# A hybrid mLSTM and attention layer: old keys copied a sequence at a time, products without sigmoids beside the gates, a reciprocal on the Pool engine, and the fourth sum of x on VectorE

## The chip, the cores and the metric

The kernel runs on one core of one Trainium2 chip. A core has a tensor engine for matmuls (TensorE, PE in the profile, with PEld for its weight loads), a vector engine (VectorE, DVE), a scalar engine (ScalarE, ACT), a general engine (GpSimd, POOL) and a sync engine that issues most transfers (SyncE, SP). The engines run side by side, each works through its own instructions in order, and they wait for each other through semaphores. The metric is the device time of one execution in microseconds (us); less is better. Times of several runs are given as a median with the lowest and the highest.

## What is computed

One layer of a decoder, for a prompt of 512 tokens and for 8 sequences with 4 new tokens each (32), so 544 columns in all. The reference, cut to what matters here:

```python
u = x @ w_in                       # 2048 wide x, 13 parts
q_m,k_m,v_m,o_m,z_m, q_a,k_a,v_a,z_a, g_m,g_a, i_pre,f_pre = split(u)
ig = i_pre + b_igate
lf = log_sigmoid(f_pre + b_fgate)  # the gates: 4 heads
h_m, C, n, m = mlstm(q_m, k_m, v_m, ig, lf, C0, n0, m0)   # cumulative sums and maxima of ig, lf
h_a = window_attention(q_a, k_a, v_a, slopes, sinks)      # window of 128, old keys from a buffer
br_m = norm(h_m) * sigmoid(o_m) * silu(z_m)
br_a = h_a * silu(z_a)
y = sigmoid(g_m) * (br_m @ w_proj_m) + sigmoid(g_a) * (br_a @ w_proj_a)
out = layernorm(alpha * x + y @ w_out)
# also returned: C, n, m, and the key and value buffers (the old rows shifted by the new ones)
```

`state_attn_k` and `state_attn_v` hold 128 old rows for each of the 8 sequences; the returned buffers hold their last 124 rows and the 4 new ones.

## The kernel before

**Products in two halves of precision.** Everything is float32, but TensorE works on a rounded form. A weight block `raw` (128 x 1024) is split into a rounded part `wh`, cast on ACT (L198), and a remainder `wl = raw - wh`, subtracted on DVE (L199); x has the same two parts. A plain product (`products`, L207) runs wh with x's high part, wh with its low part and wl with its high part.

**Pairs of products.** Nearly all of `w_in` is multiplied by `paired` (L695 on): two blocks of 128 output columns together as seven products of quarter size, the steps n = 0 to 6 of a pair, in the manner of Strassen and Winograd. Each step is 16 matmuls with wh (L662) and then 8 with wl (L664), into one of three banks. The operands on the x side are the quarters of x and four sums of them, s1, n2, n3 and s4, each in a high and a low part (s1h, s1l and so on). The operands on the weight side are blocks and sums of blocks, which `prepare` makes three steps ahead: sums on DVE (L642), or, for the pairs marked "acc", by a transfer on POOL's queue that adds as it writes (L640). `gather` takes the results out of the banks on ACT, POOL and DVE (L672 to L691): after step 1 it needs POOL for c22 (L681), after step 5 DVE for c12 (L689).

**Order of the work.** First two plain products (the values of attention, 16 + 16 steps of k) with the gates' products between them (`gates_half`, which loads the gates' columns `graw` and writes their parts `wga` and `wgb`; its two matmul lines are L388). Then a list of pairs: the keys KA first, then three from the list `fill`, then sixteen pairs QA/ZA of attention with the rest of `fill` between them. `fill` holds the first seven merge gates, whose results get a sigmoid on ACT and are stored to `d_sgm` and `d_sga`, and then the products of the mLSTM (V, K, Q), which are stored as they are.

**Side work.** `tick()` is called after each step and lets each running generator go on to its next `yield`. There are the gates' chain (`gates`), the transposes of values and keys, the sums of x (`x_sums`), and attention (`attentions`), which begins when the gates' chain has ended. `gates` computes the log sigmoid on four rows of 544 columns: absolute value and exponential on ACT, then on DVE `dd = 2 + e`, its reciprocal (L418), `s = e * dd` (L421), its square (L422), a polynomial in steps of one SCALAR_TENSOR_TENSOR each (L426, L428), then cumulative sums and maxima, exponentials on ACT, and transposes. `x_sums` makes the sums on POOL (L552, and for the fourth L572 and L573) and splits them with `hilo` (L242: a cast on ACT and a subtraction on DVE). The fourth sum `n2r` is made in place over n2 and becomes s4 behind the plain products.

**What sets the order on an engine.** A tile scheduler orders each engine's instructions by priority: the order of the program, moved ahead by `tc.high_priority(offset=...)` (400 for `prepare` and `gather`, 500 for the gates' products) and held back by `tc.issue_after(x)`, which lets work start no earlier in that order than x. So work that is moved in the program also moves other work on the same engine. POOL issues its adding transfers in order with its own operations; SP issues loads and stores in order.

**Table loads.** Where ACT goes from one function to another, the timeline can show a row ACT_TABLE_LOAD ahead of the operation; a group of them is put down to the line of that operation or of one beside it.

Of the kernel before, what the change touches and what calls it, by code (L numbers as in the profile page):

```python
# [21 lines left out]
SEQ = 512  # L22
# [51 lines left out]
def _build(tc, nc, i, o, es):  # L74
# [35 lines left out]
    def r32(ap):  # L110
        return ap.bitcast(F32)
# [172 lines left out]
    def two_k(ch):  # L284
        return slice(ch * 2, ch * 2 + 2)
# [65 lines left out]
    with tc.issue_after(state["load"].ins):  # L351
# [5 lines left out]
        nc.sync.dma_start(sinkb[:], i["attn_sinks"].partition_broadcast(128))  # L357
        nc.sync.dma_start(sinkc[:], i["attn_sinks"].unsqueeze(1).to_broadcast([AH, NTS]))
    G.memset(mh[:], -0.5)
    V.tensor_scalar(ones_r[:], cc[:, 0:2], 0.0, 0.5, op0=ALU.mult, op1=ALU.add)  # L360
    A.copy(sel[:], cc[:, C_SEL:C_SEL + 32])
    for t_ in (row_h, nM):
# [28 lines left out]
    def gates(ps):  # L391
# [23 lines left out]

        dd, s, s2, p, lf = row(), u, u2, row(), row()
        V.tensor_scalar(dd, e_, 2.0, None, op0=ALU.add)
        V.reciprocal(dd, dd)  # L418
        yield
        yield  # L420
        V.tensor_tensor(out=s, in0=e_, in1=dd, op=ALU.mult)  # L421
# [10 lines left out]
        yield  # L432

        rst, c = s, s2
        G.memset(rst, 1.0)
        G.memset(rst[:, 0:SEQ:128], 0.0)
        G.memset(rst[:, SEQ:T:NTS], 0.0)
        V.tensor_tensor_scan(c, rst, lf, 0.0, ALU.mult, ALU.add)
        ap, d0 = lf, row()
        V.tensor_tensor(out=ap, in0=ig, in1=c, op=ALU.subtract)  # L440
        yield
        G.memset(d0, 0.0)
        V.tensor_copy(d0[:, 128:SEQ:128], c[:, 127:SEQ - 1:128])
        V.memset(d0[:, SEQ:T:NTS], NEG)
        am, M = p, fg
# [32 lines left out]
        V.tensor_tensor(out=dc, in0=m0, in1=nMs, op=ALU.add)  # L478
        yield
        yield  # L480
        A.activation(T2[0:4], mrow, AF.Exp, scale=-1.0)
        A.activation(T2[64:68], wl_, AF.Exp)
        A.activation(T2[32:36, SEQ:T], it, AF.Exp)
        A.activation(dc, dc, AF.Exp)
        V.tensor_copy(T1[0:4, :], ap)
# [5 lines left out]
        for q in (32, 64):  # L491
            V.tensor_tensor(out=M, in0=M, in1=r32(nM[q - 32:q - 28]), op=ALU.subtract)
            A.copy(nM[q:q + 4], M)

        reps = []
        for src in (T2, T1):
# [52 lines left out]
    def x_sums():  # L549
        for ch in range(4):  # L550
            ks_ = two_k(ch)
            G.tensor_tensor(out=n2r[:, ks_], in0=n2r[:, ks_], in1=s1r[:, ks_], op=ALU.subtract)  # L552
            if ch % 2:
                yield
        for name, r_ in (("n3", n3r), ("s1", s1r), ("n2", n2r)):
            h_, l_ = S[name] = quad(act2, name)
            for ch in range(4):
                ks_ = two_k(ch)
                if name == "n3":
                    A.activation(h_[:, ks_], r_[:, ks_], AF.Copy, scale=-1.0)  # L560
                    V.scalar_tensor_tensor(l_[:, ks_], r_[:, ks_], -1.0, r32(h_[:, ks_]), op0=ALU.mult, op1=ALU.subtract)
                else:

                    with tc.issue_after(state["x_end"].ins):
                        hilo(r_[:, ks_], h_[:, ks_], l_[:, ks_])
                if ch % 2:
                    yield
        for ch in range(4):
            ks_ = two_k(ch)
            k0 = (ch * 2) % 4  # L570
            h12, l12 = (r32(xk2[p][ch // 2][:, k0:k0 + 2, 0:HT]) for p in range(2))
            G.tensor_tensor(out=n2r[:, ks_], in0=h12, in1=n2r[:, ks_], op=ALU.subtract)  # L572
            G.tensor_tensor(out=n2r[:, ks_], in0=n2r[:, ks_], in1=l12, op=ALU.add)  # L573

        while not state.get("plain_done"):
            yield
        s4 = S["s4"] = quad(act, "s4")
        for ch in range(4):
            ks_ = two_k(ch)
            hilo(n2r[:, ks_], s4[0][:, ks_], s4[1][:, ks_])  # L580
            yield

# [241 lines left out]
    def end_qz(k):  # L824
# [16 lines left out]
            waiting[k] = (qs, sz)  # L841
        return end

    def attentions():
        while gates_ in live:
            yield
        esG.close()
        with tc.issue_after(state["gates_end"].ins):
            V.tensor_scalar(nsinkb[:], sinkb[:], -1.0, None, op0=ALU.mult)
        with tc.issue_after(state["load"].ins):  # L850
            for src, dst in ((d_ks, kb_s), (d_vr[SEQ:T], vb_s)):
                nc.sync.dma_start(dst[:, 124:128].rearrange("b t k d -> b t (k d)"),
                                  src.rearrange("(b t) c -> b t c", t=NTS))
            nc.sync.dma_start(kb_s[:, 0:124], i["state_attn_k"][:, NTS:128])
            nc.sync.dma_start(vb_s[:, 0:124], i["state_attn_v"][:, NTS:128])
        state["ca"] = pool(esP, "ca", 1).tile([128, 388], F32, name="ca")
        with tc.issue_after(state["load"].ins):
            nc.sync.dma_start(state["ca"][:], i["consts"][:, C_DIST:C_DIST + 388])
        open_attention()
        state["open"] = True  # L860
        for k in range(16):
            if k % 4 == 0:
                kv = kv_head(k // 4)
            while k not in waiting:
                yield
            yield
            yield
            yield from attention(k, *waiting.pop(k), kv)
            state["done"] = k + 1
        esB.close()  # L870
        yield from sample_attention()
        esT.close()
        esP.close()
        open_samples()
        state["samples"] = True
# [394 lines left out]

    merge_gates = [pair(GA + ct * 128, GM + ct * 128, end_gates(d_sga, ct, d_sgm, ct)) for ct in range(16)]

    fill = merge_gates[:7] + [w for h in range(2) for w in vkq(h)]
    work = [pair(KA, KA + 128, end_keys)] + [fill.pop(0) for _ in range(3)]
    n_fill = len(fill)
    for k in range(16):
# [585 lines left out]
```

## Time and profile before

| | us |
|---|---|
| median of 3 runs | 2508.42 (2507.06 to 2509.03) |
| the profiled execution, its own time | 2510.34 |
| its span in the profile | 2508.6 |
| mean granted clock of TensorE | 0.997 |

The span reaches from the first to the last instruction that the profiler recorded; the execution's own time is 1.7 us longer. In the page's second part the span is cut into 40 slices of 62.7 us, and a digit is the busy share in tenths:

```profile
PE   8999999999999999999999999999999999999997
DVE  7867677677677677787777888787855654766667
ACT  5557676667667665443433444444633333344431
POOL 5111121121111111121111122211000000110101
```

POOL is used most in the first slice, in which the sums of x are made. Lines of a timeline give the start and the duration in us, the engine, the line of the program, the operation, what it writes and reads, the shape, the count, and in brackets the idle time ahead of it and what ended it. A row of busy time by stage gives the stretch, its length, then for PE, PEld, DVE, ACT and POOL the busy time with the count of instructions, the granted clock, the DMA share and GB/s.

### The profile page before, as it was taken

The numbers are of one execution on the slowest core, as the hardware profiler recorded it, in microseconds if no ns is written. First come the engines' busy times: TensorE is split into PE (matmuls) and PEld (weight loads), VectorE is DVE, ScalarE is ACT, GpSimd is POOL, SyncE is SP. The second block draws the span as 40 slices with busy tenths as digits, with TensorE's granted clock in tenths as the row PEclk, the third lists the DMA queues.
The fourth block names the chain that finished last, engine by engine and source line by source line (L and its number), as shares of the span: only waits on it lengthen the run. The fifth ranks groups of instructions, "written<-read, shape, count | busy, mean of one in ns | idle before, by whom it ended". The sixth has DMA issues, their size and how long they took to land.

```text
span 2508.6 us, 48661 instructions
## 1 busy us (share of the span) xinstructions
PE 2469.9 (98%) x19542; PEld 2411.2 (96%) x19542; DVE 1815.4 (72%) x2773; ACT 1244.6 (50%) x2035; POOL 402.5 (16%) x388
## 2 busy tenths in 40 slices
PE   8999999999999999999999999999999999999997
PEld 7999999999999999999999999999999999999997
DVE  7867677677677677787777888787855654766667
ACT  5557676667667665443433444444633333344431
POOL 5111121121111111121111122211000000110101
PEclk9999999999999999999999999999999999999999
DMA  6676666666666655467667567576745546788776
GB/s 165 152 199 159 158 145 163 152 151 159 153 154 156 152 126 150 106 202 227 193 211 226 164 199 217 172 220 216 247 160 177 188 153 212 209 228 251 209 216 195
DMA packets 551331, 457.35 MB, mean 182 GB/s; under 512 B 44832, under 2 KB 451536, under 8 KB 550816
## 3 DMA queue, kind: packets, MB, share of 16 engines
q1 hardware_dynamic: 534208, 394.73, 53.1%
q0 software_dynamic: 15696, 57.15, 11.7%
q8 instruction: 153, 2.51, 0.4%
q10 hardware_dynamic: 1200, 2.36, 0.3%
q14 instruction: 74, 0.61, 0.1%
HBM read 313.82 MB, written 94.22 MB: 163 GB/s over the span
## 4 chain that ended last, share of the span: by engine, by line
PE 85%; issue 5%; DMA 4%; DVE 2%; ACT 1%; SPq 0%; POOL 0%; DVEq 0%; POOLq 0%; ACTq 0%
PE bank L662 43%; PE bank L664 21%; PE bank L207 6%; PE sm L1366 2%; PE sm L1186 1%; PE sm L1180 1%; PE sm L1398 1%; PE sm L770 1%; PE sm L1411 1%; PE sm L808 1%; PE sm L207 1%; PE sm L798 1%; PE sm L1728 1%; DMA tx<-d_y 1%; DVE wl L199 1%
## 5 line engine op out<-in xcount | busy, mean ns | idle before, releaser
L198 ACT CAST wh<-raw 128x1024 fp32r<-128x1024 f32 x632 | 661.4, 1048 | 815.8 <-PE bank L662 678.0
L199 DVE TENSOR_TENSOR wl<-raw,wh 128x1024 fp32r<-128x1024 f32 x632 | 779.6, 1234 | 239.7 <-ACT wh L198 207.2
L662 PE MATMUL bank<-xk,wh 128*128 128x272 f32 x2336 | 322.7, 288 | 1.7 <-ACT wh L198 1.2
L642 DVE TENSOR_TENSOR raw<-raw,raw 128x1024 f32<-128x1024 f32 x238 | 303.5, 1278 | 14.1 <-DMA raw<-in_w_in 5.4
L662 PEld LDWEIGHTS bank<-xk,wh 128*128 128x128 f32 x2336 | 303.9, 188 | 4.3 <-ACT wh L198 1.7
L681 POOL TENSOR_TENSOR ev<-p,ev 128x272 f32<-128x272 f32 x82 | 121.0, 1476 | 583.6 <-ACT ev L680 533.9
L664 PE MATMUL bank<-xk,wl 128*128 128x272 f32 x1168 | 171.7, 287 | 0.0
L662 PE MATMUL bank<-n3h,wh 128*128 128x272 f32 x656 | 169.2, 289 | 1.6 <-DVE ev L683 1.6
L662 PE MATMUL bank<-s1h,wh 128*128 128x272 f32 x656 | 170.0, 291 | 0.2 <-ACT wh L198 0.2
L662 PE MATMUL bank<-n2h,wh 128*128 128x272 f32 x656 | 168.9, 288 | 1.1 <-ACT wh L198 1.1
L662 PE MATMUL bank<-s4h,wh 128*128 128x272 f32 x656 | 169.3, 290 | 0.4
L662 PE MATMUL bank<-n3l,wh 128*128 128x272 f32 x656 | 169.0, 289 | 0.0
L662 PE MATMUL bank<-n2l,wh 128*128 128x272 f32 x656 | 168.8, 289 | 0.0
L662 PE MATMUL bank<-s1l,wh 128*128 128x272 f32 x656 | 168.5, 289 | 0.0
L662 PE MATMUL bank<-s4l,wh 128*128 128x272 f32 x656 | 168.4, 289 | 0.0
L664 PEld LDWEIGHTS bank<-xk,wl 128*128 128x128 f32 x1168 | 155.8, 188 | 0.0
L662 PE MATMUL bank<-a11h,wh 128*128 128x272 f32 x584 | 150.0, 289 | 0.2 <-ACT wh L198 0.2
L662 PE MATMUL bank<-a11l,wh 128*128 128x272 f32 x584 | 149.9, 289 | 0.0
L207 PE MATMUL bank<-bh,wl 128*128 128x272 f32 x704 | 147.5, 289 | 1.3 <-DVE wl L199 1.3
L207 PE MATMUL bank<-bl,wh 128*128 128x272 f32 x704 | 148.6, 289 | 0.0
L207 PE MATMUL bank<-bh,wh 128*128 128x272 f32 x704 | 148.1, 289 | 0.0
L640 POOL DMA_DIRECT2D raw<-raw x90 | 77.6, 863 | 302.8 <-DVE sums L783 153.0
(489 smaller groups left out, 5640.1 us busy)
## 6 DMA issues: line engine op xcount, KB each, us to landing
raw<-in_w_in SPq DMA_DIRECT2D x296, 512.0 KB, 4.7
raw<-raw POOLq DMA_DIRECT2D x90, 512.0 KB, 5.0
C<-in_state_mlstm_C SPq DMA_DIRECT2D x32, 1024.0 KB, 7.0
out<-C SPq DMA_DIRECT2D x64, 512.0 KB, 3.6
raw<-in_w_proj_a SPq DMA_DIRECT2D x32, 512.0 KB, 7.1
raw<-in_w_proj_m SPq DMA_DIRECT2D x32, 512.0 KB, 5.7
raw<-in_w_out SPq DMA_DIRECT2D x32, 512.0 KB, 5.5
d_sgm<-ev SPq DMA_DIRECT2D x16, 272.0 KB, 8.4
```

What stands on the lines that cost most here:

```text
L198: A.copy(wh[:, k:k + n], raw[:, k:k + n])
L199: V.tensor_tensor(out=wl[:, k:k + n], in0=raw[:, k:k + n], in1=r32(wh[:, k:k + n]), op=ALU.subtract)
L207: PE.matmul(ps[f][:, :w], a[:, kk], b(k, c, w), start=(k == 0 and n == 0), stop=(k == 15 and n == 2))
L640: G.dma_start(out=w[out][:], in_=w[b][:], accum_op=ALU.add)
L642: V.tensor_tensor(out=w[out][:], in0=w[a][:], in1=w[b][:], op=ALU.add)
L662: PE.matmul(ps, wh[:, k], x(p, k), start=(first and k == 0 and p == 0), stop=False, skip_group_check=True)
L664: state["end"] = PE.matmul(ps, wl[:, k], x(0, k), start=False, stop=(k == 7), skip_group_check=True)
L681: G.tensor_tensor(out=c22, in0=p1, in1=c11, op=ALU.subtract)
L770: PE.matmul(pp[:, c0 + w0:c0 + 256], qs[a][:, j * 128:j * 128 + 128], kx[:, k0:k0 + 256 - w0], start=(n == 0), stop=(n == 1))
L798: PE.transpose(pt[:, (m - m0_) * 128:(m - m0_) * 128 + 128], s_[:, b, 128:256] if own else s_[:, b + 1, 0:128], ident)
L808: PE.matmul(po[:, b * 128:b * 128 + n], VA[:, b], p_[:, 2 * b:2 * b + n // 128], start=(b == 0 and m == 0), stop=(b == 3 and m == 1), skip ...
L1366: PE.matmul(pp[:, 0:258], a[:, b * 128:b * 128 + 128], b_[:, b, f], start=(b == 0 and n == 0), stop=(b == 3 and n == 2))
```

## The change

The diff has four parts. **Old rows:** the last 124 old rows of keys and values were copied by two transfers, issued when attention opens; now a generator `old_rows` issues sixteen, one for each sequence and buffer, one in every second tick, each not ahead of the latest weight load. **Fill:** the list now begins with the mLSTM's products of heads 0 and 1, with the seven merge gates put in behind the first three; so the three pairs behind KA are V, V and K and no longer merge gates. **Gates:** the reciprocal becomes a power of -1 on POOL (a two-input operation whose second input is a column of -1.0 in `mh`, broadcast), with one more `yield` behind it; four memsets go from POOL to DVE; two exponentials change places, and a `yield` is added between the copies into `nM`. **Fourth sum:** its eight TENSOR_TENSOR go from POOL to DVE and behind the wait for the plain products' end.

```diff
@@ -357,6 +357,7 @@
         nc.sync.dma_start(sinkb[:], i["attn_sinks"].partition_broadcast(128))
         nc.sync.dma_start(sinkc[:], i["attn_sinks"].unsqueeze(1).to_broadcast([AH, NTS]))
     G.memset(mh[:], -0.5)
+    G.memset(mh[:, 4:8], -1.0)
     V.tensor_scalar(ones_r[:], cc[:, 0:2], 0.0, 0.5, op0=ALU.mult, op1=ALU.add)
     A.copy(sel[:], cc[:, C_SEL:C_SEL + 32])
     for t_ in (row_h, nM):
@@ -415,7 +416,8 @@
 
         dd, s, s2, p, lf = row(), u, u2, row(), row()
         V.tensor_scalar(dd, e_, 2.0, None, op0=ALU.add)
-        V.reciprocal(dd, dd)
+        G.tensor_tensor(out=dd, in0=dd, in1=mh[0:4, 4:5].to_broadcast([4, T]), op=ALU.pow)
+        yield
         yield
         yield
         V.tensor_tensor(out=s, in0=e_, in1=dd, op=ALU.mult)
@@ -432,14 +434,14 @@
         yield
 
         rst, c = s, s2
-        G.memset(rst, 1.0)
-        G.memset(rst[:, 0:SEQ:128], 0.0)
-        G.memset(rst[:, SEQ:T:NTS], 0.0)
+        V.memset(rst, 1.0)
+        V.memset(rst[:, 0:SEQ:128], 0.0)
+        V.memset(rst[:, SEQ:T:NTS], 0.0)
         V.tensor_tensor_scan(c, rst, lf, 0.0, ALU.mult, ALU.add)
         ap, d0 = lf, row()
         V.tensor_tensor(out=ap, in0=ig, in1=c, op=ALU.subtract)
         yield
-        G.memset(d0, 0.0)
+        V.memset(d0, 0.0)
         V.tensor_copy(d0[:, 128:SEQ:128], c[:, 127:SEQ - 1:128])
         V.memset(d0[:, SEQ:T:NTS], NEG)
         am, M = p, fg
@@ -478,8 +480,8 @@
         V.tensor_tensor(out=dc, in0=m0, in1=nMs, op=ALU.add)
         yield
         yield
-        A.activation(T2[0:4], mrow, AF.Exp, scale=-1.0)
-        A.activation(T2[64:68], wl_, AF.Exp)
+        with tc.issue_after(A.activation(T2[64:68], wl_, AF.Exp).ins):
+            A.activation(T2[0:4], mrow, AF.Exp, scale=-1.0)
         A.activation(T2[32:36, SEQ:T], it, AF.Exp)
         A.activation(dc, dc, AF.Exp)
         V.tensor_copy(T1[0:4, :], ap)
@@ -491,6 +493,7 @@
         for q in (32, 64):
             V.tensor_tensor(out=M, in0=M, in1=r32(nM[q - 32:q - 28]), op=ALU.subtract)
             A.copy(nM[q:q + 4], M)
+            yield
 
         reps = []
         for src in (T2, T1):
@@ -565,18 +568,16 @@
                         hilo(r_[:, ks_], h_[:, ks_], l_[:, ks_])
                 if ch % 2:
                     yield
+
+        while not state.get("plain_done"):
+            yield
+        s4 = S["s4"] = quad(act, "s4")
         for ch in range(4):
             ks_ = two_k(ch)
             k0 = (ch * 2) % 4
             h12, l12 = (r32(xk2[p][ch // 2][:, k0:k0 + 2, 0:HT]) for p in range(2))
-            G.tensor_tensor(out=n2r[:, ks_], in0=h12, in1=n2r[:, ks_], op=ALU.subtract)
-            G.tensor_tensor(out=n2r[:, ks_], in0=n2r[:, ks_], in1=l12, op=ALU.add)
-
-        while not state.get("plain_done"):
-            yield
-        s4 = S["s4"] = quad(act, "s4")
-        for ch in range(4):
-            ks_ = two_k(ch)
+            V.tensor_tensor(out=n2r[:, ks_], in0=h12, in1=n2r[:, ks_], op=ALU.subtract)
+            V.tensor_tensor(out=n2r[:, ks_], in0=n2r[:, ks_], in1=l12, op=ALU.add)
             hilo(n2r[:, ks_], s4[0][:, ks_], s4[1][:, ks_])
             yield
 
@@ -841,6 +842,15 @@
             waiting[k] = (qs, sz)
         return end
 
+    def old_rows():
+
+        for dst, src in ((kb_s, i["state_attn_k"]), (vb_s, i["state_attn_v"])):
+            for b in range(NB):
+                with tc.issue_after(state["load"].ins):
+                    nc.sync.dma_start(dst[b, 0:124], src[b, NTS:128])
+                yield
+                yield
+
     def attentions():
         while gates_ in live:
             yield
@@ -851,13 +861,12 @@
             for src, dst in ((d_ks, kb_s), (d_vr[SEQ:T], vb_s)):
                 nc.sync.dma_start(dst[:, 124:128].rearrange("b t k d -> b t (k d)"),
                                   src.rearrange("(b t) c -> b t c", t=NTS))
-            nc.sync.dma_start(kb_s[:, 0:124], i["state_attn_k"][:, NTS:128])
-            nc.sync.dma_start(vb_s[:, 0:124], i["state_attn_v"][:, NTS:128])
         state["ca"] = pool(esP, "ca", 1).tile([128, 388], F32, name="ca")
         with tc.issue_after(state["load"].ins):
             nc.sync.dma_start(state["ca"][:], i["consts"][:, C_DIST:C_DIST + 388])
         open_attention()
         state["open"] = True
+        spawn(old_rows())
         for k in range(16):
             if k % 4 == 0:
                 kv = kv_head(k // 4)
@@ -1270,7 +1279,8 @@
 
     merge_gates = [pair(GA + ct * 128, GM + ct * 128, end_gates(d_sga, ct, d_sgm, ct)) for ct in range(16)]
 
-    fill = merge_gates[:7] + [w for h in range(2) for w in vkq(h)]
+    fill = [w for h in range(2) for w in vkq(h)]
+    fill[3:3] = merge_gates[:7]
     work = [pair(KA, KA + 128, end_keys)] + [fill.pop(0) for _ in range(3)]
     n_fill = len(fill)
     for k in range(16):
```

On DVE around the gates' products, in rows of line, operation, output, inputs and shape, before (n2l is the low part of the sum n2, ev a result on its way out, raw2 a sum of weight blocks, graw the gates' columns):

```order
L242 TENSOR_TENSOR n2l_70_723<-n2r_134,n2h_69_722 128x544 x4
L383 TENSOR_TENSOR wga_55_589<-graw_54_587,wga_55_589 128x8x4 x2
L531 COPY ev_65_703<-sm_63_696 32x128
L199 TENSOR_TENSOR wl_59_634<-raw_57_631,wh_58_633 128x1024
L642 TENSOR_TENSOR raw2_83_775<-raw_77_763,raw_78_765 128x1024
```

And after:

```order
L242 TENSOR_TENSOR n2l_70_724<-n2r_134,n2h_69_723 128x544 x4
L579 TENSOR_TENSOR n2r_134<-xk2_5_115,n2r_134 128x544
L384 TENSOR_TENSOR wga_55_590<-graw_54_588,wga_55_590 128x8x4 x2
L579 TENSOR_TENSOR n2r_134<-xk2_5_115,n2r_134 128x544
L579 TENSOR_TENSOR n2r_134<-xk2_6_116,n2r_134 128x544 x2
L580 TENSOR_TENSOR n2r_134<-n2r_134,xk2_7_117 128x544
L534 COPY ev_65_704<-sm_63_697 32x128
L199 TENSOR_TENSOR wl_59_635<-raw_57_632,wh_58_634 128x1024
L580 TENSOR_TENSOR n2r_134<-n2r_134,xk2_7_117 128x544
L580 TENSOR_TENSOR n2r_134<-n2r_134,xk2_8_118 128x544 x2
L643 TENSOR_TENSOR raw2_83_776<-raw_77_764,raw_78_766 128x1024
```

One of the fourth sum's operations now stands between the four n2l and wga, and the seven others around the split of the last plain product's weights (wl_59).

On DVE in the last steps of the first pair (KA), before: t are the gates' rows; ev_95 and ev_94 are the pair's results, with L687 after step 4, L689 after step 5 and L691 after step 6; wl_111 is the low part for step 6, and wl_115 that for the first step of the next pair:

```order
L444 MEMSET t_135_1157 4x8
L426 SCALAR_TENSOR_TENSOR t_100_882<-t_100_882,t_76_753 4x544 x2
L199 TENSOR_TENSOR wl_111_934<-raw2_80_769,wh_110_933 128x1024
L687 SCALAR_TENSOR_TENSOR ev_95_848<-bank_98_855,ev_95_848 128x272
L531 COPY ev_109_927<-sm_107_920 32x128
L426 SCALAR_TENSOR_TENSOR t_100_882<-t_100_882,t_76_753 4x544
L642 TENSOR_TENSOR raw2_116_999<-raw_104_890,raw_105_892 128x1024
L689 SCALAR_TENSOR_TENSOR ev_95_848<-bank_93_822,ev_95_848 128x272
L199 TENSOR_TENSOR wl_115_969<-raw_104_890,wh_114_968 128x1024
```

And after (L690 is the evacuation after step 5, L423 the product with the reciprocal, L444 and L446 memsets of one row, L428 steps of the polynomial):

```order
L690 SCALAR_TENSOR_TENSOR ev_95_849<-bank_93_823,ev_95_849 128x272
L423 TENSOR_TENSOR t_75_753<-t_90_815,t_99_882 4x544
L688 SCALAR_TENSOR_TENSOR ev_95_849<-bank_98_856,ev_95_849 128x272
L424 TENSOR_TENSOR t_76_754<-t_75_753 4x544
L426 TENSOR_SCALAR t_100_883<-t_76_754 4x544
L432 TENSOR_SCALAR t_101_884<-t_74_752 4x544
L444 MEMSET t_139_1191 4x544
L428 SCALAR_TENSOR_TENSOR t_100_883<-t_100_883,t_76_754 4x544
L446 MEMSET t_139_1191 4x8
L428 SCALAR_TENSOR_TENSOR t_100_883<-t_100_883,t_76_754 4x544 x3
L199 TENSOR_TENSOR wl_111_935<-raw2_80_770,wh_110_934 128x1024
```

Before, wl_111 stood ahead of the evacuation after step 5 (L689), and the product with the reciprocal, L421, stood six rows ahead of the first row shown; now wl_111 stands behind both evacuations (steps 4 and 5) and, from L423 on, ten operations of the gates' chain.

On POOL in the same stretch, from the plain products on, before (xk2 are the parts of x, raw and raw2 are weight blocks and sums, the DMA rows are issues of adding transfers):

```order
L572 TENSOR_TENSOR n2r_134<-xk2_5_115,n2r_134 128x544 x2
L572 TENSOR_TENSOR n2r_134<-xk2_6_116,n2r_134 128x544 x2
L573 TENSOR_TENSOR n2r_134<-n2r_134,xk2_7_117 128x544 x2
L573 TENSOR_TENSOR n2r_134<-n2r_134,xk2_8_118 128x544 x2
L640 DMA raw_78_765<-raw2_79_767 128x1024
L681 TENSOR_TENSOR ev_95_848<-p1_89_812,ev_94_847 128x272
L640 DMA raw2_80_769<-raw_77_763 128x1024
L442 MEMSET t_135_1157 4x544
```

And after:

```order
L377 MEMSET wga_55_590 128x1024
L378 MEMSET wgb_56_591 128x1024
L641 DMA raw_78_766<-raw2_79_768 128x1024
L419 TENSOR_TENSOR t_99_882<-t_99_882,mh_88 4x544
L682 TENSOR_TENSOR ev_95_849<-p1_89_813,ev_94_848 128x272
L641 DMA raw2_80_770<-raw_77_764 128x1024
L458 MEMSET t_146_1265 128x544
```

The sum's operations (L572, L573) are gone from POOL, and the power, L419, stands between the adding transfer for step 4's block, raw_78, and c22 (L682), with the adding transfer for step 6's block, raw2_80, behind both.

4 lines of the change are left out of this document (2 added, 2 removed).

## The prediction

> **What bounds the kernel now.** I read the page first (busy time by engine), then busy time by stage, then what PE waited for, and last the timelines around those waits.
>
> ```profile
> span 2508.6 us, 48661 instructions
> PE 2469.9 (98%) x19542; PEld 2411.2 (96%) x19542; DVE 1815.4 (72%) x2773; ACT 1244.6 (50%) x2035; POOL 402.5 (16%) x388
> ```
>
> TensorE (PE) is busy for all but 38.7 us. An edit that leaves the matmuls alone can only close such holes or open new ones, so the question is where the holes are. By stage (PE's busy time is the third number, PEclk the granted clock):
>
> ```profile
> 45.00:48.70 3.70, 0.15 (x3) 0.06 (x1) 3.70 (x6) 0.93 (x2) 3.70 (x3) 1.00 0.00 0
> 49.50:53.00 3.50, 3.50 (x18) 3.50 (x17) 1.35 (x2) 0.00 (x0) 3.50 (x3) 0.51 0.98 263
> 60.00:95.00 35.00, 34.86 (x279) 34.60 (x278) 31.09 (x42) 16.99 (x23) 7.43 (x11) 1.00 0.61 147
> 95.00:120.00 25.00, 21.70 (x163) 20.38 (x162) 20.84 (x40) 15.51 (x22) 2.64 (x4) 1.00 0.63 149
> 144.00:160.00 16.00, 14.04 (x108) 13.41 (x107) 10.44 (x16) 7.68 (x12) 2.41 (x3) 1.00 0.85 204
> 160.00:2300.00 2140.00, 2136.25 (x17003) 2085.56 (x17002) 1558.99 (x2367) 1091.68 (x1775) 332.53 (x315) 1.00 0.65 181
> 2446.00:2508.60 62.60, 45.93 (x322) 44.26 (x320) 44.80 (x81) 8.63 (x12) 7.17 (x8) 0.91 0.64 195
> ...
> PE bank L388 <- DVE wga L383: 3.5, 1, 3.5
> PE bank L662 <- ACT wh L198: 2.7, 5, 1.1
> PE bank L662 <- DVE ev L683: 1.6, 2, 1.0
> ```
>
> Up to 160 us there are three holes the change can reach: one of 3.5 us at 45, 3.3 us (25.00 - 21.70) between 95 and 120, and 2.0 us between 144 and 160. Behind the first the clock falls to 0.51 for 3.5 us. From 160 to 2300 PE misses 3.75 us of 2140, and the end (16.7 us) lies behind work that the change does not touch. So at best about 10 us, 0.4%, are to be had, and any new hole counts against them. Between 60 and 95 PE misses 0.1 us: there is only something to lose there.
>
> **The fourth sum on VectorE.** These are DVE, PE and POOL around the first hole.
>
> ```profile
> 42.26 4.93 DVE L242 TENSOR_TENSOR n2l<-n2r,n2h 128x544 fp32r<-128x544 f32 x4
> 47.11 1.41 DVE L383 TENSOR_TENSOR wga<-graw,wga 128x32 fp32r<-128x32 f32 x2
> 59.60 1.34 DVE L242 TENSOR_TENSOR s4l<-n2r,s4h 128x544 fp32r<-128x544 f32 x2
> ...
> 48.67 0.49 PE L388 MATMUL bank<-xk,wga 128*128 128x272 f32 x2 [3.55 <-DVE wga L383]
> ...
> 27.10 1.36 POOL L344 TENSOR_TENSOR r<-n2r,r 128x544 f32<-128x544 f32 x1
> 43.12 6.62 POOL L572 TENSOR_TENSOR n2r<-xk,n2r 128x544 f32<-128x544 f32 x4 [0.40 <-ACT wgb L382]
> 49.71 8.25 POOL L573 TENSOR_TENSOR n2r<-n2r,xk 128x544 f32<-128x544 f32 x4
> ```
>
> PE waits for wga, which stands on DVE behind four n2l. They take 4.93 us while POOL adds, though the same operation takes 0.67 us each (1.34 for two) once POOL is done; POOL's own adds take 1.65 and 2.06 us against 1.36. The two engines slow each other. With POOL's eight adds gone, four n2l end at 42.3 + 2.6 = 44.9; the one moved sum that stands ahead of wga adds 0.65 us, wga at most the 1.4 us of its row: 47.0, and PE starts at 47.1 and not 48.7. **Gain 1.6 us** (0.9 if n2l stays at half of its surplus, 2.3 if wga is halved too). The other seven sums (4.6 us) stand ahead of products that PE reaches 5 us later and more; wl of the next product, first needed 16 matmuls after that, has to wait for four of them and still comes in time. What is late next is that wl: a further 0.5 us would show.
>
> The 32 matmuls after the hole took 54.28 - 48.67 = 5.6 us by the next row's start; at full rate (the row of 16 below, 0.126 us each) they take 4.0. A hole of 1.8 us later in the program was followed by no such dip:
>
> ```profile
> 54.28 0.67 PE L207 MATMUL sm<-xk,wh 128*128 128x272 f32 x4
> 159.42 2.02 PE bank L662 x16
> 2344.95 0.52 PE L207 MATMUL bank<-yh,wl 128*128 128x272 f32 x2 [1.79 <-DVE wl L199]
> 2347.00:2350.50 3.50, 3.50 (x30) 3.50 (x29) 3.50 (x7) 1.48 (x3) 0.00 (x0) 1.00 1.03 230
> ```
>
> The hole left over (45.1 to 47.1) is near the one without a dip: **gain 1.6 us** (from 0).
>
> **Products without sigmoids, keys a sequence at a time.** The holes from 95 to 160 came from ACT changing tables beside the gates and from a store that was slow in landing:
>
> ```profile
> 105.76 1.28 ACT L1239 ACT_TABLE_LOAD   x1
> 109.23 1.28 ACT L482 ACT_TABLE_LOAD   x1
> 112.89 1.28 ACT L1239 ACT_TABLE_LOAD   x1
> ...
> 145.06 0.44 DVE L683 SCALAR_TENSOR_TENSOR ev<-bank,p 128x272 f32<-128x272 f32 x1 [6.10 <-DMA d_sgm<-ev]
> DMA to landing us min/median/max: 14.8/14.8/14.8
> ```
>
> Those three loads (3.8 us) leave this stretch with the sigmoids; the sigmoids come back seven products later, beside attention, where PE waits for nothing. The copy of the old keys and values was issued just ahead of that store and delayed it to 14.8 us; in sixteen pieces it is spread, with sixteen issues on SP in place of two, ahead of loads that are used several steps later. **Gain: at most 5.3 us**, at least 0. I take all of it and put 1.0 us back for waits that stay (DVE and POOL still hold the gates' chain there).
>
> **The reciprocal on POOL.** It frees 3.5 us of DVE at a place where PE waits for nothing, so it gains nothing itself. What it moves is the rest of the gates' chain and the transfer behind it. In the changed order DVE runs the evacuation of step 5 of the first pair, then the product with the reciprocal and eight more operations of the chain, and then wl of step 6; before, wl of step 6 stood ahead of that evacuation. Since DVE works in order, wl cannot begin until step 5 has ended.
>
> ```profile
> L199 DVE TENSOR_TENSOR wl<-raw,wh 128x1024 fp32r<-128x1024 f32 x18 | 21.7, 1208 | 3.1 <-PE bank L664 1.9 <-ACT wh L198 1.1
> L426 DVE SCALAR_TENSOR_TENSOR t<-t,t 4x544 f32<-4x544 f32 x6 | 4.2, 705 | 0.0
> L418 DVE RECIPROCAL t<-t 4x544 f32<-4x544 f32 x1 | 3.5, 3543 | 0.0
> L689 DVE SCALAR_TENSOR_TENSOR ev<-bank,ev 128x272 f32<-128x272 f32 x2 | 0.9, 428 | 0.0
> L421 DVE TENSOR_TENSOR t<-t,t 4x544 f32<-4x544 f32 x1 | 0.8, 815 | 0.0
> L424 DVE TENSOR_SCALAR t<-t 4x544 f32<-4x544 f32 x1 | 0.4, 425 | 0.0
> ```
>
> Two evacuations 0.9, L421's product 0.8, its square and four steps of the polynomial 5 x 0.7, two scalings 0.85, the memset of 544 columns 0.4 (by the scaling's row; from 0.07 to 0.7), wl 1.2: 7.65 us, less some 0.3 for overlapping starts: 7.35. Against that PE has 16 matmuls of step 6 and 9 of the next pair, 25 x 0.126 = 3.15. **Loss 4.2 us** (3.7 to 4.9). A hole as long as the one of 3.55 will bring the clock down again: **loss 1.6 us** (0 if it falls in two parts).
>
> The Trainium skill, in "TensorE: Matmul & The Clock Gate", section "Why this matters for your kernels", says that a gap of more than about 3 us between matmuls puts the array back to half rate; the rows at 48.67 and 2344.95 agree with it, and by it the loss is charged, while without it the sum would be 1.6 us lower.
>
> Behind it DVE is late for the next pair: one step of the polynomial, one wl, the sum of two weight blocks and ACT's cast (0.65 + 1.15 + 1.2 + 1.05 = 4.05 us) against 23 matmuls (2.9), then a second wl: **loss 1.15 + 0.55 = 1.7 us** (0 to 2.5).
>
> How long the power takes no row shows for 544 columns. The rows around it:
>
> ```profile
> L1021 POOL TENSOR_TENSOR lns<-lns,mh x20: 547/548/1484, 1233.0 to 2049.2; 128x1 f32<-128x1 f32 x16, 32x1 f32<-32x1 f32 x4
> 92.48 0.76 POOL L681 TENSOR_TENSOR ev<-p,ev 128x272 f32<-128x272 f32 x1 [9.24 <-DMA d_ks<-ev]
> 65.48 1.05 ACT L198 CAST wh<-raw 128x1024 fp32r<-128x1024 f32 x1 [1.07 <-PE bank L662]
> 78.88 0.29 PE L662 MATMUL bank<-xk,wh 128*128 128x272 f32 x1
> DMA to landing us min/median/max: 4.5/4.7/5.2
> ```
>
> Below it is bounded by a plain add of 544 columns, 1.36 us, above by 544 times the power of one column, 544 x 0.547 = 298 us. I take 6.8 us: the reciprocal costs DVE 5 times a plain operation of its size (3543 to 705 ns), and 5 x 1.36 = 6.8.
>
> On before's clock the power begins at 67.5: the cast of step 3's weights (65.48 + 1.05), then the exponential and the sum that it now stands behind. Behind it on POOL stand c22 (0.76) and the accumulating transfer for step 6 (4.7), then ACT's cast (1.05): wh of step 6 is ready at 74.1 + P. PE reaches step 6 at 78.9, and wl is ready 7.35 later, at 86.2. With 25 matmuls to do first, wh may be as late as 83.0: **up to P = 8.9 us the power hides behind the wait for wl, beyond it every microsecond is one of PE's.**
>
> The Trainium skill, in "GPSIMD Engine Reference", section "Engine selection", gives two-input elementwise work as about twice slower there than on VectorE; twice 3.54 is an estimate of 7.1 us, by which the sum would be the same; the adds here take 1.36 against 0.67, which agrees, and no run here shows a wide power.
>
> **Sum**: -1.6 - 1.6 - 5.3 + 1.0 + 4.2 + 1.6 + 1.7 = 0.0 us. The profiled execution took 2510.3 us (span 2508.6 and 1.7 around it), 1.9 above the median of the runs. The same distance kept, the forecast is 2508.4 us. About 0.2%, 5 us, is what a measurement of this kernel can tell from no change.
>
> **Rivals.** First, slower: the power takes long. Its place is POOL between the first pair's steps 2 and 6, its price is P - 8.9 us, and from P = 13.9 it is slower by the bound: at 20 us 2519.5, at 35 us 2534.5. For it speaks that one column already costs 0.39 us more than an add's fixed part (0.76 less 272 x 2.2 ns leaves 0.16), against it that POOL's plain adds cost 2.2 ns a column once started. Chance 0.36. Second, faster: the holes close wholly (2.3 + 1.6 + 5.3 = 9.2) and the new one costs 3.7 with no dip and no backlog: -5.5, 2502.9. Against it speaks DVE, 31.1 of 35 us busy between 60 and 95. Chance 0.17. Third, the change does not do what it says: the table loads come back into the 95 to 120 stretch, or wga does not come sooner. Then 5.3 or 3.2 of the gains fall out, about 2513; chance 0.02, counted with slower by half. The forecast has 0.45.
>
> So faster has 0.17, no change 0.46, slower 0.37. From 2501 to 2535 takes in the ends of the small terms and a power of up to 35 us; what lies beyond, up to the bound of 298, and below has 0.2. Between cases the likeliest one reaches from 2503.5 to 2513.
>
> **What would show it.** PE's wait for wga of about 2 us, and the clock at 1.0 behind it; POOL's row of the power, to be set against 8.9; PE waiting 4 us or more for wl at step 6 of the first pair; no table load between 95 and 120; the copies landing without a store of 14.8 us beside them. I am wrong if PE does not wait in the stretch from 60 to 95, or if it waits there much longer than 10 us.

## The result, and the profile after

| kernel | median of 5 runs, us | lowest to highest | ratio to before, 95% interval |
|---|---|---|---|
| before | 2508.42 | 2507.06 to 2509.48 | |
| changed | 2579.78 | 2578.98 to 2580.92 | 1.0285 (1.027 to 1.030) |

The changed kernel is 71 us slower. The forecast was no change, 2508.4 us, with a range from 2501 to 2535. The page of the profiled execution (busy time by engine, then the busy tenths of 40 slices of 64.5 us):

```profile
span 2578.0 us, 48672 instructions
PE 2468.2 (96%) x19542; PEld 2412.4 (94%) x19542; DVE 1815.7 (70%) x2784; ACT 1243.5 (48%) x2033; POOL 474.8 (18%) x378
PE   8159999999999999999999999999999999999997
POOL 2941112111111111122112122212100000110111
PEclk9679999999999999999999999999999999999999
```

PE's busy time is that of before (2469.9 us); the span is 69.4 us longer. The second and third slice hold the loss: in the second PE nearly stands still and POOL is full, in the third it is so for about half of the slice. POOL's timeline and the waits of PE and DVE name it (in the timeline start and duration; in the waits who waited for whom, the sum, how many times and the longest):

```profile
65.31 87.19 POOL L419 TENSOR_TENSOR t<-t,mh 4x544 f32<-4x544 f32 x1 [9.14 <-DVE t L418]
```

```profile
PE bank L663 <- ACT wh L198: 82.0, 1, 82.0
...
DVE t L423 <- POOL t L419: 75.3, 1, 75.3
```

The power on POOL takes 87.19 us where the forecast took 6.8. PE's one wait, 82.0 us, is put down to ACT's cast, which is only the last link; the chain that ended last shows the others:

```profile
73.12 79.36 issue
152.48 0.70 POOL ev L682
153.19 4.35 DMA raw<-raw
...
157.64 1.05 ACT wh L198
...
158.73 5.80 PE bank L663 x25
```

Read it from the end: step 6 waited for its cast, the cast for the adding transfer, the transfer for its place on POOL behind c22 (L682), and c22 for the power. The 79.36 us of "issue" are c22 standing behind the power on an engine that works in order: no semaphore says so, only POOL's timeline does. The stages around it (length, then busy time of PE, PEld, DVE, ACT and POOL, the granted clock, DMA share, GB/s):

```profile
45.00:48.70 3.70, 2.96 (x25) 2.71 (x24) 3.70 (x8) 1.56 (x3) 0.00 (x0) 1.00 0.01 2
76.50:158.80 82.30, 0.29 (x3) 0.07 (x1) 6.54 (x12) 1.56 (x3) 78.37 (x5) 0.51 0.04 10
158.60:162.10 3.50, 3.37 (x15) 3.37 (x16) 3.50 (x5) 1.03 (x2) 0.00 (x0) 0.50 0.53 150
```

The first hole, at 45 us, nearly closed: PE is busy for 2.96 of 3.70 us where it was busy for 0.15. Behind the long wait the clock is at half for a while. DVE's timeline at the first hole says why it closed:

```profile
44.18 2.63 DVE L242 TENSOR_TENSOR n2l<-n2r,n2h 128x544 fp32r<-128x544 f32 x4
46.73 0.72 DVE L579 TENSOR_TENSOR n2r<-xk,n2r 128x544 f32<-128x544 f32 x1
47.37 0.28 DVE L384 TENSOR_TENSOR wga<-graw,wga 128x32 fp32r<-128x32 f32 x2
```

Four n2l take 2.63 us and not 4.93, two wga 0.28 and not 1.41. To see where else time came and went, the start of PE's n-th matmul is set against the same matmul's number in the kernel before (from the two traces, us; negative is earlier):

```
n (its start before)     200 (36.4) 300 (54.2) 470 (75.4) 520 (81.6) 600 (91.6) 1100 (162.7) 7500 (952.8) 19500 (2485.1)
changed                     +1.94      -2.40      -2.33     +82.25     +82.37       +73.98       +73.89       +69.80
reciprocal on VectorE       +0.01      -4.32      -3.20      -0.25      +0.14        -3.24        -3.30        -5.53
sum alone                   +0.67      -3.70      -2.58      +0.44      +0.84        -0.54        -0.75        -3.83
fill alone                  +0.10      +0.10      +0.10      +0.17      +0.17        -1.19        -1.40        -3.51
old rows alone              -0.07      -0.25      -0.25      -0.03      -0.03        -2.57        -2.77        -4.16
power alone                 +1.81      +1.81      +1.86     +83.17     +83.17       +79.11       +78.91       +75.08
power of 64 columns         +0.33      -4.02      -3.95      +2.99      +3.01        -3.86        -3.81        -5.09
VectorE, own buffer         +0.27      -4.07      -2.95      -2.24      -2.23        -6.69        -6.90        -9.49
```

The other rows are those of the experiments. The changed kernel gains 4.3 us at the first hole (from +1.94 to -2.40), loses 84.6 at step 6 of the first pair and gains 8.4 from there to the 1100th matmul. The power alone gains 4.1 in the same stretch (+83.17 to +79.11) with none of the other edits, so about half of the 8.4 comes with the wait itself, which lets the other engines catch up. From 163 to 953 nothing moves. What comes after that, some 1 to 4 us in every kernel of the table, lies behind the last product that an edit moves, and the profiled execution of before was itself 1.9 us above its median; it is not counted as a gain. The changed kernel and the power alone are 1.9 and 1.8 us late at the 200th matmul already. Both had one step of 3.4 us at half clock near the start, here the changed kernel's, with 18 matmuls where 29 fit at full clock:

```profile
13.94:17.36 3.42, 3.42 (x18) 3.42 (x17) 1.07 (x3) 2.15 (x10) 1.35 (x1) 0.50 1.12 335
```

The kernels with a power of 272 or of 64 columns begin with the same work and had no such step, so nothing here shows that the change brings it about.

### The profile page after: what moved, and what is told of

It reads as the page before. It is cut to its first block, busy times and chain, and to the rows that moved or that the text cites. A ratio compares the mean times of both kernels' runs of the same rounds, so it can differ in the third digit from the quotient of the medians.

```text
span 2578.0 us, 48672 instructions
## 1 busy us (share of the span) xinstructions
PE 2468.2 (96%) x19542; PEld 2412.4 (94%) x19542; DVE 1815.7 (70%) x2784; ACT 1243.5 (48%) x2033; POOL 474.8 (18%) x378
## 4 chain that ended last, share of the span: by engine, by line
PE 90%; issue 4%; DMA 3%; DVE 2%; ACT 1%; POOL 0%; SPq 0%; DVEq 0%; POOLq 0%; ACTq 0%
PE bank L663 44%; PE bank L665 22%; PE bank L207 10%; PE sm L1376 2%; PE sm L1195 1%; PE sm L1189 1%; PE sm L1408 1%; PE sm L771 1%; PE sm L1421 1%; PE sm L809 1%; PE sm L207 1%; PE sm L799 1%; DMA raw<-in_w_in 1%; PE sm L1738 1%; DMA tx<-d_y 1%
## 5 line engine op out<-in xcount | busy, mean ns | idle before, releaser
L682 POOL TENSOR_TENSOR ev<-p,ev 128x272 f32<-128x272 f32 x82 | 121.4, 1481 | 573.2 <-ACT ev L681 536.3
```

What stands on the lines that cost most here:

```text
L682: G.tensor_tensor(out=c22, in0=p1, in1=c11, op=ALU.subtract)
```

## The experiments

The kernels of a group ran on one chip beside the kernel before, whose median went from 2508.4 to 2512.1 us between chips, so ratios are compared.

### The power taken away, alone, and halved

Reciprocal back on VectorE, all else as in the change:

```diff
-        G.tensor_tensor(out=dd, in0=dd, in1=mh[0:4, 4:5].to_broadcast([4, T]), op=ALU.pow)
-        yield
+        V.reciprocal(dd, dd)
```

> The changed kernel with the reciprocal back on VectorE (the power, its column of -1 and its extra yield are gone; all else of the change stays). Theory A, the power is all that costs: the wait of 82.0 us goes, and so does the slow clock behind it (25 matmuls took 5.6 us there against 3.15 at full rate, 2.5 us); holes that the stall swallowed may come back, at most the 5.3 us of before. 2579.8 - 82.0 - 2.5 = 2495.3, up to 2500.6 us. Theory B, the other edits cost something too and the long wait hid it: 2505 us or more, with a wait of 3 us or more on TensorE somewhere between 45 and 160 us.

2504.94 us against 2512.12, ratio 0.9972 (0.996 to 0.9984). The loss is gone, so the power is its cause: 3.1% lie between the two kernels, 78.5 us on 2508.4. On 2508.4 that is 2501.4, 0.8 above what theory A gives at most and 3.6 below theory B. PE's waits up to 300 us show that something else costs, though no wait reaches B's 3 us:

```profile
PE bank L661 <- ACT wh L198: 3.3, 3, 1.8
PE bank L661 <- DVE ev L686: 1.4, 1, 1.4
PE bank L663 <- DVE wl L199: 0.8, 1, 0.8
```

The 4.3 us gained at the first hole are lost again by the 600th matmul (the table: -4.32, then +0.14). What one of the waits is follows further down.

The power alone, in the kernel before (the diff's line for L419 and the column of -1, nothing else):

> The kernel before with one edit, the reciprocal made as a power on the Pool engine. Theory A, the power costs the same by itself: 87 us on POOL, TensorE waits about 82 us for the weights of step 6 and then runs 2.5 us slower; the holes of 5.3 us behind it are swallowed: 2508.4 + 82 + 2.5 - 5.3 = 2587.6 us. Theory B, it is long in the changed kernel because of what the other edits put beside it: well under 70 us on POOL and under 2575 us.

2586.36 us, ratio 1.0297 (1.0283 to 1.0311). POOL's row and PE's longest wait:

```profile
67.17 87.19 POOL L419 TENSOR_TENSOR t<-t,mh 4x544 f32<-4x544 f32 x1 [6.45 <-DVE t L418]
```

```profile
PE bank L663 <- ACT wh L198: 80.4, 3, 79.7
```

The same 87.19 us: the power costs what it costs with or without the other edits, and theory B falls. The wait is 2.3 us shorter than in the change: the first hole is still there, so PE comes to step 6 at 80.9 and not at 76.7, and the power begins 1.9 us later. Theory A's 2587.6, 1.0316, is 5 us too high.

Half of it, the first 272 columns by the reciprocal:

```diff
+        V.reciprocal(dd[:, 0:HT], dd[:, 0:HT])
+        G.tensor_tensor(out=dd[:, HT:T], in0=dd[:, HT:T], in1=mh[0:4, 4:5].to_broadcast([4, HT]), op=ALU.pow)
```

> The changed kernel with the first 272 columns by the reciprocal on VectorE and the last 272 by the power on POOL. Theory A, the power is paid by the column (87.19 us / 544 = 0.160 us each): 43.7 us on POOL, the wait of TensorE is P - 5.2 = 38.5 us, 2579.8 - 43.5 = 2536.3 us. Theory B, most of it is paid once (a first use that loads something): over 70 us on POOL, over 2560 us.

2540.00 us, ratio 1.0112 (1.0098 to 1.0126), which on 2508.4 is 2536.5: theory A. Durations of the power (ns) and PE's row behind it:

```profile
L420 POOL TENSOR_TENSOR t<-t,mh x1: 43751/43751/43751, 63.5 to 63.5; 4x272 f32<-4x272 f32 x1
```

```profile
113.51 2.86 PE L664 MATMUL bank<-xk,wh 128*128 128x272 f32 x11 [38.57 <-ACT wh L198]
```

(87.19 - 43.75) / 272 = 0.160 us a column; what is left over, 0.3 us, is paid once. The wait is again P, the power's duration, less 5.2.

### What remains of the sum when the power is short

A multiplication in its place (the reciprocal is left out):

> The changed kernel with a multiplication by the column of -1 in place of the power on POOL: the reciprocal is left out, everything else and the order on each engine stays as in the change. POOL's operation takes 1.4 to 2.1 us. Theory A, my sum without the power: TensorE waits some 4.2 us at step 6 of the first pair for wl, which stands behind the gates' chain on VectorE, the clock falls for 3.4 us, and VectorE is 1 to 2 us late in the next pair: with the first hole down to 0.7 us about 2505 to 2509 us. Theory B, wl is not late there, since the chain is through earlier: 2495 to 2500 us as with the reciprocal on VectorE.

2500.93 us, ratio 0.9957 (0.9944 to 0.9969). POOL's row:

```profile
63.45 1.08 POOL L419 TENSOR_TENSOR t<-t,mh 4x544 f32<-4x544 f32 x1 [9.14 <-DVE t L418]
```

The multiplication reads the same broadcast column and takes 1.08 us, so it is the power and not the way its second input is read that costs. The time is theory B's, but not for its reason, and the expectation's premise was wrong: with only this operation changed, the scheduler put wl of step 6 ahead of the evacuation after step 5, where the change has it behind, so this run says nothing on that order. It does show that with nothing of the reciprocal on either engine 10.8 us are to be had.

The order of the change was kept to the end of the first pair by a power over 64 columns (the other 480 stay without a reciprocal):

```diff
-        G.tensor_tensor(out=dd, in0=dd, in1=mh[0:4, 4:5].to_broadcast([4, T]), op=ALU.pow)
+        G.tensor_tensor(out=dd[:, 0:64], in0=dd[:, 0:64], in1=mh[0:4, 4:5].to_broadcast([4, 64]), op=ALU.pow)
```

> The changed kernel with the power over the first 64 columns alone; for the other 480 the reciprocal is left out. Each engine's order is that of the changed kernel until the first pair has ended. By the two lengths measured (43.75 us for 272 columns, 87.19 for 544: 0.160 us a column and 0.3 once) the power takes 10.5 us. Theory A, what the changed kernel's trace gives, a wait of P - 5.2 us and nothing else: TensorE waits 5.3 us for wh of step 6, then runs 2.5 us slower, wl is no longer late behind it; with the gains of the other edits (10.5 us) the time is 2.7 us below the kernel before, 0.9989. Theory B, the sum of my prediction (up to 8.9 us of power hidden, a loss of 4.2 for wl, the clock and VectorE's backlog beside it): 1.7 us above the kernel before, 1.0007, with a wait for wl of several us at step 6.

2504.66 us against 2510.06, ratio 0.9979 (0.9968 to 0.999). Theory A holds, B's 1.0007 lies outside. The timelines of POOL, DVE and PE at step 6, and two stages behind it:

```profile
63.69 10.57 POOL L419 TENSOR_TENSOR t<-t,mh 4x64 f32<-4x64 f32 x1 [9.16 <-DVE t L418]
75.14 0.44 DVE L690 SCALAR_TENSOR_TENSOR ev<-bank,ev 128x272 f32<-128x272 f32 x1 [0.86 <-PE bank L665]
81.31 1.21 DVE L199 TENSOR_TENSOR wl<-raw,wh 128x1024 fp32r<-128x1024 f32 x1
80.51 3.53 PE L663 MATMUL bank<-xk,wh 128*128 128x272 f32 x16 [5.41 <-ACT wh L198]
```

```profile
80.00:83.40 3.40, 2.89 (x13) 2.89 (x14) 3.37 (x5) 1.41 (x2) 0.00 (x0) 0.51 0.61 154
83.40:86.80 3.40, 3.40 (x29) 3.40 (x29) 3.40 (x4) 1.05 (x1) 0.86 (x1) 1.00 0.00 0
```

The wait is 5.41 us, as the other two lengths foretold. wl of step 6 ends at 82.5. Had wh been there when step 5 ended (80.51 - 5.41 = 75.1), PE would have asked for wl after 25 matmuls, at 78.2, and waited 4.3 us: the forecast's 4.2. Here the wait for wh covers it. Nor is DVE late behind it: the table stays at +3.0 from the 520th to the 600th matmul.

### The three other edits, each alone

> The kernel before with one edit, the fourth sum of x on VectorE behind the plain products. Theory A, the term of the prediction with the first hole as the changed kernel shows it: the wait for wga falls from 3.55 to 0.7 us and the clock does not dip behind it, -2.8 - 1.6 = -4.4 us, 0.9982 of the kernel before. Theory B, VectorE pays it back: it is as loaded from 60 to 95 us as with the reciprocal on VectorE and the whole change, where TensorE had waits of 0.8, 1.1 and 1.4 us for it; -4.4 + 3.2 = -1.2 us, 0.9995.

2507.25 us against 2510.06, ratio 0.9993 (0.9982 to 1.0004): theory B by the trace, though the interval takes in both. The waits of PE up to 300 us:

```profile
PE bank L659 <- ACT wh L198: 4.4, 4, 2.5
PE bank L659 <- DVE ev L684: 1.6, 1, 1.6
PE bank L661 <- DVE wl L199: 1.2, 2, 0.8
```

It gains 4.4 us at the first hole (+0.67 to -3.70), as expected, and has lost them by the 520th matmul (+0.44).

> The kernel before with one edit, the products without sigmoids ahead of the merge gates. Theory A, the term of the prediction: ACT's three table loads leave the stretch from 95 to 120 us and TensorE's holes of 3.3 us there go for the most part, -2 to -3.3 us, 0.9987 to 0.9992 of the kernel before; if the slow store falls elsewhere too, -5.3, 0.998. Theory B, the holes there come from VectorE and the transfers, not from the tables: 0.9996 or more, with the holes of that stretch still over 2 us in sum.

2507.87 us, ratio 0.9994 (0.9985 to 1.0003). No table load is left between 60 and 173 us, and 2.2 us are gained between the 700th and the 800th matmul (+0.50 to -1.69, by the traces), 1.4 net of what is lost before and after. From 95 to 120 us PE still misses 1.95 of the 3.3 us. 0.5 is lost again where DVE waits for a store:

```profile
143.43 0.44 DVE L683 SCALAR_TENSOR_TENSOR ev<-bank,p 128x272 f32<-128x272 f32 x1 [5.83 <-DMA d_v<-ev]
```

It is another store now, d_v for d_sgm, behind the same two copies. So the tables cost something there, as theory A has it, but the holes do not go for the most part, and the ratio lies between the two theories with an interval that takes in both. The slow store doesn't go with the tables.

> The kernel before with one edit, the old keys and values copied in sixteen transfers, one in every second tick. Theory A, the term of the prediction: no store takes 14.8 us in landing, TensorE's holes of 2.0 us between 144 and 160 go, -2 us, 0.9992 of the kernel before. Theory B, the store is late for another reason or the sixteen copies slow the weight loads: 1.000 or more.

2506.64 us, ratio 0.9988 (0.9979 to 0.9997). The stage with the store, and how long the stores of d_sgm took to land:

```profile
144.00:160.00 16.00, 16.00 (x130) 16.00 (x129) 10.55 (x13) 9.14 (x13) 0.85 (x1) 1.00 0.93 245
```

```profile
DMA to landing us min/median/max: 2.0/3.3/4.7
```

PE misses nothing there where it missed 2.0 us, and no store takes 14.8 us: theory A. By the table 2.6 us are gained up to the 1100th matmul. The three together, 0.9993, 0.9994 and 0.9988, give 0.9975, and the change with the reciprocal on VectorE 0.9972.

### Why the sum's gain was lost again

With the reciprocal on VectorE, DVE stood still while it was needed:

```profile
78.08 0.28 DVE L532 COPY ev<-sm 32x128 f32<-32x128 f32 x1 [3.57 <-DMA out<-ev]
...
80.05 0.42 DVE L686 SCALAR_TENSOR_TENSOR ev<-bank,ev 128x272 f32<-128x272 f32 x1
```

A small copy of the values waits for a buffer that a store still holds, and the evacuation that PE needs (L686) stands behind it. In the kernel before the same copy waited 1.35 us, behind that evacuation. The next kernel gives it a buffer of its own:

```diff
-        vr, vs = ev(512), ev(128)
+        vr, vs = ev(512), cst.tile([128, 128], F32, name=nm("vs"))
```

> The changed kernel with the reciprocal back on VectorE, and with a buffer of its own for the small copy of the values (vs, written by VectorE) that took one of the three ev buffers. Theory A: with the reciprocal on VectorE that copy stood 3.57 us on VectorE until a store had let go of its buffer, the evacuation after step 4 stood behind it, and TensorE's holes of 1.07 and 1.35 us at 77 and 80 us come from that; without the wait they go: 9.5 us below the kernel before (7 of them measured without this edit), 0.9962. Theory B, VectorE is simply full there: the holes stay or move, 0.997 as without the edit.

2501.53 us against 2510.41, ratio 0.9967 (0.9954 to 0.9979). DVE no longer waits there, and of PE's holes at 77 and 80 us one row is left:

```profile
76.53 0.39 PE L661 MATMUL bank<-a11h,wh 128*128 128x272 f32 x1 [0.42 <-ACT wh L198]
```

By the trace theory A holds (2 us of holes gone: -2.23 at the 600th matmul against +0.14); the ratios with and without the buffer overlap and don't tell them apart. Some 1.8 us of the gain at the first hole are still lost by then (-4.07 to -2.23), and no run shows to what. Its ratio is the lowest of the kernels here that leave nothing out; it is faster than before and than the change.

> As the run with the reciprocal on VectorE and a buffer for vs, and with the four memsets of the gates' chain back on POOL. Theory A, VectorE has room: no difference from the run without this, 0.996 to 0.997. Theory B, VectorE is full from 60 to 95 us: 1.0 us less, 0.4 per thousand.

2502.87 us, ratio 0.997 (0.9957 to 0.9982). No difference from the run before it is seen, as theory A has it, but the interval takes in theory B's 0.4 per thousand too.

### What the power is paid by

Powers of several shapes on a buffer of their own:

> The changed kernel with the reciprocal on VectorE and, on a buffer that nothing else uses, powers on POOL of 4 x 64, 128 x 64, 128 x 17, 4 x 17, 128 x 1 with exponent -1, 4 x 64 with exponent -0.5, one multiplication of 4 x 64, and a reciprocal of 128 x 17 on VectorE. They only have to show their durations; the time of the whole is of no use. Theory A, the power is paid by the column whatever the number of rows and the exponent: 10.6 us for all three of 64 columns, 3.1 us for both of 17, 0.5 us for one. Theory B, it is paid by the element: 128 x 64 takes tens of times as long as 4 x 64. Theory C, the exponent -0.5 goes another way: it differs from -1 by more than a tenth.

Rows of POOL's timeline (the first counts two, of 4 x 64 and of 128 x 64; the fourth, of 4 x 64, has the exponent -0.5; the last is a multiplication), and a reciprocal on DVE:

```profile
1.62 21.16 POOL L1844 TENSOR_TENSOR pq<-pq,mh 4x64 f32<-4x64 f32 x2
29.79 3.56 POOL L1844 TENSOR_TENSOR pq<-pq,mh 128x17 f32<-128x17 f32 x1
39.58 3.53 POOL L1844 TENSOR_TENSOR pq<-pq,mh 4x17 f32<-4x17 f32 x1
44.87 10.68 POOL L1844 TENSOR_TENSOR pq<-pq,mh 4x64 f32<-4x64 f32 x1
61.10 0.90 POOL L1844 TENSOR_TENSOR pq<-pq,mh 128x1 f32<-128x1 f32 x1
62.08 0.28 POOL L1845 TENSOR_TENSOR pq<-pq,mh 4x64 f32<-4x64 f32 x1
62.40 0.27 DVE L1846 RECIPROCAL pq<-pq 128x17 f32<-128x17 f32 x1 [2.68 <-POOL pq L1845]
```

Theory A: 64 columns take 10.5 to 10.7 us, whatever the rows and the exponent. The short ones take 0.4 us more than expected.

## Why the prediction was wrong

**The step that failed** is one term: "I take 6.8 us: the reciprocal costs DVE 5 times a plain operation of its size (3543 to 705 ns), and 5 x 1.36 = 6.8." The power took 87.19 us, 13 times that, and 24.6 times the reciprocal. A ratio between two operations of one engine was carried to another operation on another engine. The rule of the Trainium skill set beside it ("GPSIMD Engine Reference", section "Engine selection", about twice VectorE) speaks of plain two-input work; it agrees with the adds (1.36 against 0.67 us) and does not hold for the power. The row that could have told was quoted: one column, 0.547 us. The text took off 0.16 for an add's fixed part and had 0.39 left, but used it only as an argument for a rival. Read as a price by the column, it gives 0.16 + 544 x 0.39 = 212 us, too much by 2.4, and a loss all the same. The upper bound, 298, was right; the range was cut at a power of 35 us for no reason from a row. The rival had the place, the sign and the form.

**From P on the steps hold.** Place: POOL between steps 2 and 6 of the first pair, as written. Price: one for one. The text had wh ready at 74.1 + P and PE there at 78.9, a wait of P - 4.8; measured is P - 5.2, at 10.57, 43.75 and 87.19 us alike. The wait for wl that it covers was 4.2 by the forecast and 4.3 by the run of 64 columns. With 87.19 put into the sum it gives 2508.4 + 78.3 = 2586.7, against 2579.8 measured.

**The 6.9 us between them, term by term.** The first hole and its dip: 3.2 forecast, 4.3 measured; the hole came down to 0.73 and not to 2.0, as n2l kept no surplus and wga took a fifth of its row. DVE's backlog: 1.7 forecast, none measured (+82.25 to +82.37 from the 520th to the 600th matmul), since DVE works while PE waits. The holes from 95 to 160: 5.3 less 1.0 forecast, 8.4 measured. The power alone gains 4.1 there, so as much came with the wait, for which the forecast had no term; what is left, 4.3, is near what it gave the two edits. That the wait could give so much is seen in before, where the views differ: PE's busy time misses 3.3 us from 95 to 120, but its 163 matmuls there are some 35 short of what the rate further on gives (17003 in 2140 us, 199 in 25), 4.5 us, and the 108 from 144 to 160 some 19 short, 2.4 us. Those 4.5 and 2.4 stand against 3.3 and 2.0 read as holes of busy time. The slow clock behind the wait: 1.6 forecast, some 2.5 measured. The loss at step 6: 78.3 + 4.2 forecast, a wait of 82.0 measured. Together 1.1 + 1.7 + 4.1 - 0.9 + 0.5 = 6.5 of the 6.9; the rest is within what two executions differ by.

**What was right for the wrong kernel.** That the fourth sum's seven other operations cost nothing holds here because PE stands still; with the sum alone, or with the reciprocal on VectorE, the gain is lost by 92 us, partly to a copy on DVE that waits for a store's buffer. The forecast saw DVE full there and charged it to the gates' chain. The two gains ascribed to tables and to the copies are seen in the traces, 2.2 (1.4 net) and 2.6 us, against 3.3 and 2.0 forecast; by the ratios only the copies' is clear of no change.

**Without the power** the other edits are worth 0.28% (0.9972), at the edge of what can be told from no change; with one more buffer 0.33%.

## What to carry to other kernels

Before an operation goes to another engine, find its price there by the column, from two sizes if the profile has them, and treat one small size as a slope and not as an overhead; where only one is at hand, keep the whole bound in the range. An engine that works in order makes a long operation the wait of everything queued behind it, and the profile then shows the last link (a cast) and "issue", so read the queue's own timeline. An operation paid by the column on 4 rows wants its data on 128: the same 2176 elements take 0.27 us as 128 x 17 on VectorE and 3.54 as 4 x 544. No run here laid the gates' rows out so, and bringing them there has a price of its own.

## What the runs showed of the hardware that was not expected

The power on POOL costs 0.160 us a column and 0.3 us once at 64, 272 and 544 columns (10.57, 43.75 and 87.19 us), at 64 columns nearly the same on 4 rows as on 128 and for -0.5 as for -1.

The clock fell behind some holes far shorter than 3 us, and not behind some longer ones. In the traces' records the granted clock changes in steps of 3.413 us: in the changed kernel its stretches before the end are 1, 2, 18, 25 and 704 such steps long. Stages set at the edges of these steps, counted from the nearest change of the clock, show two holes of the kernel with the reciprocal on VectorE. The first row holds one of 1.82 us, the third one of 1.90:

```profile
100.37:103.78 3.41, 1.59 (x13) 1.37 (x12) 3.10 (x4) 1.99 (x2) 0.00 (x0) 1.00 0.56 127
103.78:107.19 3.41, 3.41 (x18) 3.41 (x17) 3.38 (x6) 0.00 (x0) 0.00 (x0) 0.50 0.90 262
2336.10:2339.51 3.41, 1.63 (x14) 1.40 (x12) 3.00 (x5) 1.33 (x5) 0.93 (x1) 1.00 0.71 235
2339.51:2342.93 3.42, 3.30 (x26) 3.30 (x27) 3.18 (x10) 1.94 (x4) 0.00 (x0) 1.00 1.08 162
```

With the sum alone a hole of 2.50 us lies across an edge, and the clock stays at 1.00 in the step behind these two as well:

```profile
99.85:103.26 3.41, 1.93 (x16) 1.71 (x14) 2.15 (x4) 1.02 (x2) 0.00 (x0) 1.00 0.46 90
103.26:106.68 3.42, 2.40 (x19) 2.40 (x20) 3.31 (x6) 2.92 (x5) 0.00 (x0) 1.00 1.04 276
```

Where PE was busy for 1.59 of 3.41 us the next step ran at half (18 matmuls against 26); at 1.63, and at 1.93 with 2.40, it did not. Counted so over all 13 traces, every step at full clock with PE busy for 1.60 us or less was followed by one at half, and of those with 1.63 or more only two were, both at 10 us (1.83 in the power alone, 2.24 in the changed kernel). So the share of one step seems to decide, a little under half, and not the length of the hole; why the two at 10 us differ stays open, and no run moved a hole against the steps to test it. The rule of about 3 us that the prediction drew on (the Trainium skill, "TensorE: Matmul & The Clock Gate", "Why this matters for your kernels") fits the holes of 3.55 and 5.41 us and not that of 1.82; the same page's Part 1 speaks of windows of 3413 ns that run freely, which agrees with the steps.
